# The hidden tiles of both FFNs start 128 bytes higher in SBUF

## The chip, the cores and the metric

The kernel runs on one core of one Trainium2 chip. The metric is the device time of one execution in microseconds (us); the number for the kernel before is the median of three runs. A profile of one execution gives the start and duration of every instruction on each engine: TensorE (PE for the matmuls, PEld for the weight loads), VectorE (DVE), ScalarE (ACT), GpSimd (POOL) and the queue that issues transfers (SP).

## What is computed

One layer of a hybrid streaming encoder on 512 tokens of width 1024, in float32. It is a macaron block: a half-weighted feed-forward network (FFN), a mixer with two kinds of attention heads, an output projection, a second half-weighted FFN, and a final norm.

```python
x = x + 0.5 * swiglu(rmsnorm(x, ffn1_norm), ffn1_w_gate, ffn1_w_up, ffn1_w_down)
proj = rmsnorm(x, mix_norm) @ w_in
...
x = x + concatenate([out_a, out_b]) @ w_out
x = x + 0.5 * swiglu(rmsnorm(x, ffn2_norm), ffn2_w_gate, ffn2_w_up, ffn2_w_down)
x = rmsnorm(x, final_norm)

def swiglu(h, w_gate, w_up, w_down):
    return (silu(h @ w_gate) * (h @ w_up)) @ w_down
```

The hidden width of an FFN is 2816, so it has 22 tiles of 128; the model width has 8 tiles of 128.

## The kernel before

Everything is held with features on the 128 partitions and the 512 tokens along the row, so that a tile of activations is 128 x 512 float32 values, 2,048 bytes in each partition. To keep float32 accuracy, each operand is split into a high and a low part (`xh`/`xl`, `x2h`/`x2l`, `h1h`/`h1l`, `h2h`/`h2l` for activations, `whi`/`wlo` for weights), and each product of 128 x 128 weights with 128 x 512 activations is three matmuls, issued by the helper `mm3` at lines 151 to 153: high x high, high x low and low x high (stationary x moving). The weights are the stationary operand, the activations the moving one (they stream through the array). In the projections `pj` (line 314), `uq` and `ukv` of the mixer it is the other way round: a 128-column piece of activations or latents stands still, and the weights move.

Weights arrive by transfer into `raw`, a block of up to 1,024 columns at a time; ScalarE makes `whi` (line 146), and GpSimd, or VectorE in a few places, makes `wlo` (line 147). Four buffers of each rotate.

The stages around the change, in the order of the program:

- FFN 1, gate and up (`gu`): for each of the 22 hidden tiles, 2 x 8 products on `xh`/`xl`, that is 1,056 matmuls. `gate` (lines 162 to 168) turns them into `h1h[f]`, `h1l[f]`.
- FFN 1, down (`dn`): for each of 8 output tiles, 22 products on `h1h`/`h1l`, 528 matmuls.
- The mixer: input projections `pj`, query and key/value projections `uq` and `ukv` from the latents `latT`, scores `s`, transposes `t` and `tr`, weighted values `pv`.
- The output projection (`wo`): 8 x 8 products on `xh`/`xl`, 192 matmuls.
- FFN 2, gate and up: 1,056 matmuls on `x2h`/`x2l`.
- FFN 2, down: as in FFN 1, but of its 22 hidden tiles only the first 14 are `h2h`/`h2l`; the last 8 are put into `xh`/`xl`, which are free by then. So one output tile is 42 matmuls on `h2` tiles, then 24 on `xh`/`xl`. The last output tile is done in two halves of 256 columns, which lets the final norm start early.

**Where the tiles lie.** Pools of SBUF are stacked in the order in which they are opened: `const`, `wpool`, `work`, `small`, and then, one after another at the same base, the pool of FFN 1 (`h1`), of the mixer (`mix`) and of the output projection with FFN 2 (`h2`). A tile takes its row in bytes, rounded up to 32. The tiles of `const` start at byte 16,512 of a partition. From there the sizes give, for the kernel before:

| tiles | first byte | remainder of 256 | remainder of 512 |
|---|---|---|---|
| `xh0` to `xl7` (16 tiles of 2,048) | 32,896 | 128 | 128 |
| `raw`, `whi`, `wlo` (4 buffers of 4,096 each) | 71,040, 87,424, 103,808 | 128 | 384 |
| `wa`, `wb`, `wc` of `work` (2,048 each) | 120,192 | 128 | 384 |
| first tile of `h1`, `mix` and `h2` | 132,864 | 0 | 256 |
| `h1h0`, `h1l0`, `h1h1`, ... and `x2h0`, ..., `x2l7`, `h2h0`, `h2l0`, ... (2,048 each) | from 132,864 | 0 | 256 |
| `latT` in `mix` (6 rows of 2,048) | 161,536 | 0 | 256 |

Within a weight tile, a block of 128 columns begins every 512 bytes. In the first projection of the mixer (416 columns) the second block of a weight tile begins 1,664 bytes on, which is 128 past a multiple of 256.

The order of instructions on each engine is set by a scheduler when the program is built.

Of the kernel before, what the change touches and what calls it, by code (L numbers as in the profile page):

```python
# [10 lines left out]
F32 = mybir.dt.float32  # L11
# [6 lines left out]
P = 128  # L18
# [5 lines left out]
NT = S // P  # L24
# [7 lines left out]

# columns of the packed parameter array
C_FFN1, C_MIX, C_FFN2, C_FINAL = 0, 8, 16, 24
# [5 lines left out]
def tile_macaron_block(  # L40
# [24 lines left out]

# [1 line left out]
    x = [const.tile([P, S], F32, name=f"x{k}") for k in range(KD)]  # L67
# [29 lines left out]

# [1 line left out]
    def split_x(k, c):  # L99
# [13 lines left out]
    def rsqrt(out, v, y, y2):  # L113
        """out = v^-1/2: by logarithm and exponential, then one Newton step."""
        act.activation(y, v, AF.Ln)
        act.activation(y, y, AF.Exp, scale=-0.5)
        dve.tensor_tensor(out=y2, in0=y, in1=y, op=ALU.mult)
        dve.tensor_tensor(out=y2, in0=y2, in1=v, op=ALU.mult)
        dve.tensor_scalar(out=y2, in0=y2, scalar1=-0.5, scalar2=1.5, op0=ALU.mult, op1=ALU.add)
        dve.tensor_tensor(out=out, in0=y, in1=y2, op=ALU.mult)  # L120

    def rstd_rows(ps):
        """rs[:, n] = (mean_d x[d, n]^2 + eps)^-1/2 on every partition."""
        sh = work.tile([P, S], F32R, tag="wa", name="sh")
        sl = work.tile([P, S], F32R, tag="wa", name="sl")
        act.copy(sh, ssum)
        dve.tensor_tensor(out=sl, in0=ssum, in1=sh.bitcast(F32), op=ALU.subtract)
        m = ps.tile([P, S], F32, tag="mm", name="ms")
        pe.matmul(m, lhsT=ones, rhs=sh, start=True, stop=False)
        pe.matmul(m, lhsT=ones, rhs=sl, start=False, stop=True)  # L130
        v = work.tile([P, S], F32, tag="wb", name="v")
        y = work.tile([P, S], F32, tag="wa", name="y")
        y2 = work.tile([P, S], F32, tag="wc", name="y2")
        dve.tensor_scalar(out=v, in0=m, scalar1=EPS, scalar2=None, op0=ALU.add)
        rsqrt(rs, v, y, y2)

    def wunit(src, n, lo_on=None, raw=None, step=1024):
        """A block of weights, split: hi + lo, both exact in 12 bits."""
        if raw is None:
            raw = wpool.tile([P, 1024], F32, tag="raw", name="raw")  # L140
            nc.sync.dma_start(out=raw[:, :n], in_=src)
        hi = wpool.tile([P, 1024], F32R, tag="whi", name="whi")
        lo = wpool.tile([P, 1024], F32R, tag="wlo", name="wlo")
        for c in range(0, n, step):
            cc = slice(c, min(n, c + step))
            act.copy(hi[:, cc], raw[:, cc])  # L146
            (lo_on or pool).tensor_tensor(out=lo[:, cc], in0=raw[:, cc], in1=hi[:, cc].bitcast(F32), op=ALU.subtract)  # L147
        return hi, lo
# [6 lines left out]
    def ffn(ps, gu, dn, H, XH, XL, after, raw0=None, squares=None, last=None):  # L155
        def gate(f, gup):
            """h = silu(g) u = (g / 2) (tanh(g / 2) + 1) u, split."""
            gs = work.tile([P, S], F32, tag="wa", name="gs")
# [54 lines left out]

    # =====================================================  FFN 1
    with tc.tile_pool(name="h1", bufs=1, reuse_waits="tile") as hp, \
            tc.tile_pool(name="ps1", bufs=8, space=PSUM, reuse_waits="tile") as ps:
        H = [(hp.tile([P, S], F32R, name=f"h1h{f}"), hp.tile([P, S], F32R, name=f"h1l{f}")) for f in range(NF)]
        # the tensor engine's clock rises while the first loads are under way
        warm = ps.tile([P, S], F32, tag="mm", name="warm")
# [16 lines left out]

    # =====================================================  mixer
    AH, AL = XH, XL
    with tc.tile_pool(name="mix", bufs=1, reuse_waits="tile") as mp:
# [14 lines left out]
        nc.sync.dma_start(out=rgain, in_=rope_gain)  # L254
        # rtab[:, q/k, t, :]: cos*g1, sin*g2, sin*g1, cos*g2
        rtmp = mp.tile([P, 2560], F32, tag="vAl", name="rtmp")
# [10 lines left out]
        def factors(ss, n, width, scaled, name):  # L267
            """ss [P, NT, n] sums of squares -> factors of the RMS norm, rtok folded in where scaled."""
            f = mp.tile([P, NT, n], F32, tag="f_" + name, name="f_" + name)
# [12 lines left out]
        def rope(dst, src, fac, i, n, tmp):  # L282
            """src [P, NT, n, 32] * fac -> normalised, rotated, into dst (gains in rtab)."""
            xn, a, b = tmp[:, :, :, 0:32], tmp[:, :, :, 32:48], tmp[:, :, :, 48:64]
# [12 lines left out]
        with tc.tile_pool(name="ps2", bufs=1, space=PSUM, reuse_waits="tile") as ps:  # L297
            NB = {"s": 2, "tr": 2, "t": 3, "pv": 1}

            def bank(group, i, name):  # L300
                """Bank i of one of the two groups of four."""
                tag = (("s",) * NB["s"] + ("tr",) * NB["tr"], ("t",) * NB["t"] + ("pv",) * NB["pv"])[group][i]
                return ps.tile([P, 512], F32, tag=tag, name=name, bufs=NB[tag])

            def in_proj(off, n, group):
                """The columns off.. of W_in for all tokens: four banks, one per token tile."""
                pts = [bank(group, t, "pj") for t in range(NT)]
# [9 lines left out]
            def sumsq(src, ss, nh, width):  # L317
                """ss[.., h] = sum of squares over each group of width columns of src."""
                sq = work.tile([P, 512], F32, tag="wb", name="sqp")
                sv = sq[:, :nh * width].rearrange("p (h w) -> p h w", w=width)  # L320
                act.activation(sv, src, AF.Square)
                dve.tensor_reduce(out=ss, in_=sv, op=ALU.add, axis=AX.X)

            # latents, with the token statistics
            pts = in_proj(0, LAT, 1)
# [44 lines left out]

            # B: queries from their latents
            qB = mp.tile([P, NT, NH, QK], F32, tag="qB", name="qB")
# [23 lines left out]

            # B: keys and values from their latents
            ssk = mp.tile([P, NT, NH], F32, tag="ssk", name="ssk")
# [26 lines left out]

# [1 line left out]
            def values_proj():  # L427
                """A: values."""
                VAh = mp.tile([P, NT, 4, 192], F32R, tag="vAh", name="VAh")
# [14 lines left out]
            def transposes(src):  # L444
                """The four token tiles of src(t) [128, n], transposed into one bank [n, 512]."""
                pt = ps.tile([P, 512], F32, tag="tr", name="tr", bufs=NB["tr"])
# [12 lines left out]
            def front(h):  # L459
                """Transposed, scaled and split queries and keys of a head (A: of its pair)."""  # L460
                if h < NH:
# [36 lines left out]
            def softmax(qh, ql, kh, kl, bias):  # L498
                """Probabilities of the query tiles 3..0, on 128 (i + 1) keys each."""
                pa = wpool.tile([P, 1024], F32, tag="raw", name="pa")  # L500
# [7 lines left out]
                for i, so in ((3, s3), (2, s2), (1, s01[:, 256:512]), (0, s01[:, 0:256])):  # L508
                    n = (i + 1) * P
# [10 lines left out]
            def flip(pi):  # L520
                """Probabilities with the keys on the partitions, split: keys 0 | keys 1 and keys 2 | keys 3."""
                t0 = ps.tile([P, 512], F32, tag="t", name="t0", bufs=NB["t"])
# [32 lines left out]

            # the stages of four neighbouring heads overlap
            shared["V"] = values_proj()
# [12 lines left out]

    # =====================================================  output projection, FFN 2, final norm
    with tc.tile_pool(name="h2", bufs=1, reuse_waits="tile") as hp, \
            tc.tile_pool(name="ps4", bufs=7, space=PSUM, reuse_waits="tile") as ps:
        X2H = [hp.tile([P, S], F32R, name=f"x2h{k}") for k in range(KD)]
        X2L = [hp.tile([P, S], F32R, name=f"x2l{k}") for k in range(KD)]
# [18 lines left out]

        # final norm: per half of the tokens, rstd as columns, spread over the partitions by the tensor engine
        mt = ps.tile([P, 512], F32, tag="mt", name="mt", bufs=1)
# [10 lines left out]
        def means(h):  # L607
            """The mean squares of these tokens in columns, with the last tile's part."""
            act.activation(sq[:, h], x[k7][:, h], AF.Square)
# [45 lines left out]
def _kxm(w, kt, m):  # L655
    """[kt*128, m] -> [128, kt, m]: the rows of each k tile on the partitions."""
    return w.reshape(kt, P, m).transpose(1, 0, 2)
# [10 lines left out]
def _layout(i):  # L668
# [16 lines left out]
    out["rope_tab"] = _rope_table()  # L685
    # the bias of query p and key column c of a tile whose last 128 columns are the query's own block
    rel = np.clip(np.arange(P)[:, None] + (S - P) - np.arange(S)[None, :], -128, 128) + 128
# [33 lines left out]
```

## Time and profile before

| what | value |
|---|---|
| median of three runs | 1017.27 us (1016.59 to 1018.25) |
| the profiled execution, first to last instruction (its own time; the page gives no other) | 1016.7 us |
| TensorE, matmuls | 993.1 us busy, 4579 instructions |
| TensorE, weight loads | 813.7 us |
| GpSimd | 591.5 us |
| VectorE | 397.3 us |
| ScalarE | 387.6 us |

A matmul's duration in the profile runs from its start to a modelled end behind the next one's start, so the durations of matmuls in a row overlap. How fast they follow one another is read from their starts, or from how many start in a stretch of known length. A window's count takes in an instruction that had begun before its edge.

### The profile page before, as it was taken

Reading aid. Unit: us, or ns where it says so; the run is one execution under the profiler, and the core shown is the slowest. Engines: PE = TensorE matmul, PEld = TensorE weight load, DVE = VectorE, ACT = ScalarE, POOL = GpSimd, SP = SyncE. Lnnn points to the kernel's source line nnn. Section 1 sums busy time; section 2 is a strip of 40 time slices with the busy share of each in tenths; the row PEclk is TensorE's granted clock in tenths of the full one; section 3 lists DMA queues with packets and bytes.
Section 4 is the critical chain, followed back from the end, with each engine's and each line's share of the span. In section 5 each row is a group of like instructions: output and inputs, shape, how many; then the busy total and the mean of one; then the engine's idle time right before and its main releaser. Section 6 shows DMA issues by size and latency. Waiting matters only on the chain.

```text
span 1016.7 us, 12060 instructions
## 1 busy us (share of the span) xinstructions
PE 993.1 (98%) x4579; PEld 813.7 (80%) x4579; DVE 397.3 (39%) x687; ACT 387.6 (38%) x648; POOL 591.5 (58%) x429
## 2 busy tenths in 40 slices
PE   7999999999999999898999999999999999999996
PEld 4888888888888889786778978888888888888886
DVE  7534324323121224776788845143333332200002
ACT  4433323323222225663678853343232332222220
POOL 7586676676555521285355567586666656645540
PEclk7999999999999999998999999999999999999999
DMA  5423323323333333220010062323322332333302
GB/s 201 151 83 105 104 83 104 104 83 94 97 94 93 91 110 104 83 62 1 21 43 2 1 208 86 101 84 103 95 92 86 101 102 80 90 103 94 99 16 83
DMA packets 28714, 89.90 MB, mean 88 GB/s; under 512 B 3440, under 2 KB 5616, under 8 KB 28656
## 3 DMA queue, kind: packets, MB, share of 16 engines
q1 hardware_dynamic: 27504, 88.08, 27.8%
q10 hardware_dynamic: 1152, 1.05, 0.3%
q8 instruction: 36, 0.59, 0.2%
q14 instruction: 22, 0.18, 0.1%
HBM read 87.02 MB, written 2.10 MB: 88 GB/s over the span
## 4 chain that ended last, share of the span: by engine, by line
PE 88%; DVE 4%; POOL 2%; issue 2%; ACT 1%; DMA 1%; POOLq 0%; DVEq 0%; ACTq 0%; SPq 0%
PE gu L153 16%; PE gu L152 16%; PE gu L151 16%; PE dn L151 8%; PE dn L152 8%; PE dn L153 8%; PE pj L153 2%; PE pj L151 2%; PE pj L152 2%; PE wo L153 1%; PE wo L152 1%; PE wo L151 1%; PE t L533 1%; PE s L151 1%; PE tr L448 1%
## 5 line engine op out<-in xcount | busy, mean ns | idle before, releaser
L147 POOL TENSOR_TENSOR wlo<-raw,whi 128x1024 fp32r<-128x1024 f32 x138 | 323.3, 2344 | 159.3 <-ACT whi L146 159.3
L146 ACT CAST whi<-raw 128x1024 fp32r<-128x1024 f32 (+3 forms) x165 | 167.3, 1014 | 468.1 <-PE gu L152 263.6
L152 PE MATMUL gu<-xl,whi 128*128 128x512 f32 x352 | 139.2, 396 | 3.0 <-DVE xl L101 2.9
L151 PE MATMUL gu<-xh,whi 128*128 128x512 f32 x352 | 138.3, 393 | 1.5 <-ACT whi L146 1.5
L151 PE MATMUL gu<-x2h,whi 128*128 128x512 f32 x352 | 139.0, 395 | 0.0
L153 PE MATMUL gu<-x2h,wlo 128*128 128x512 f32 x352 | 138.9, 395 | 0.0
L152 PE MATMUL gu<-x2l,whi 128*128 128x512 f32 x352 | 138.9, 395 | 0.0
L153 PE MATMUL gu<-xh,wlo 128*128 128x512 f32 x352 | 138.4, 393 | 0.2 <-DVE wlo L147 0.2
L166 POOL TENSOR_TENSOR us<-us,gs 128x512 f32<-128x512 f32 x44 | 58.4, 1329 | 111.8 <-DVE us L164 110.0
L165 DVE SCALAR_TENSOR_TENSOR gs<-th,gs 128x512 f32<-128x512 f32 x44 | 90.1, 2052 | 31.7 <-ACT th L163 31.7
L162 DVE TENSOR_TENSOR gs<-gu,rs 128x512 f32<-128x512 f32 x44 | 30.4, 691 | 178.5 <-PE gu L153 171.3
L199 DVE SCALAR_TENSOR_TENSOR x<-dn,x 128x512 f32<-128x512 f32 (+1 forms) x17 | 11.2, 661 | 198.9 <-PE dn L153 198.9
L152 PEld LDWEIGHTS gu<-xl,whi 128*128 128x128 f32 x352 | 66.6, 189 | 20.3 <-DVE xl L101 7.0
L151 PEld LDWEIGHTS gu<-xh,whi 128*128 128x128 f32 x352 | 66.8, 190 | 15.9 <-ACT whi L146 1.9
L151 PEld LDWEIGHTS gu<-x2h,whi 128*128 128x128 f32 x352 | 66.1, 188 | 16.1
L152 PEld LDWEIGHTS gu<-x2l,whi 128*128 128x128 f32 x352 | 66.1, 188 | 16.1
L153 PEld LDWEIGHTS gu<-x2h,wlo 128*128 128x128 f32 x352 | 66.1, 188 | 16.0
L153 PEld LDWEIGHTS gu<-xh,wlo 128*128 128x128 f32 x352 | 66.8, 190 | 14.5 <-DVE wlo L147 1.1
L153 PE MATMUL dn<-h1h,wlo 128*128 128x512 f32 x176 | 69.5, 395 | 0.0
L151 PE MATMUL dn<-h1h,whi 128*128 128x512 f32 x176 | 69.5, 395 | 0.0
L152 PE MATMUL dn<-h1l,whi 128*128 128x512 f32 x176 | 69.5, 395 | 0.0
L164 DVE SCALAR_TENSOR_TENSOR us<-gu,rs 128x512 f32<-128x512 f32 x44 | 30.4, 690 | 69.0 <-PE gu L153 65.5
(318 smaller groups left out, 1830.4 us busy)
## 6 DMA issues: line engine op xcount, KB each, us to landing
raw<-in_gu SPq DMA_DIRECT2D x87, 512.0 KB, 3.6
raw<-in_dn SPq DMA_DIRECT2D x32, 512.0 KB, 3.5
raw<-in_dn SPq DMA_DIRECT2D x16, 384.0 KB, 3.1
raw<-in_w_in SPq DMA_DIRECT2D x12, 512.0 KB, 3.5
raw<-in_w_out SPq DMA_DIRECT2D x8, 512.0 KB, 4.2
x<-in_xT SPq DMA_DIRECT2D x8, 256.0 KB, 5.2
bias<-in_bias_tab SPq DMA_DIRECT2D x8, 256.0 KB, 2.7
raw<-in_w_in SPq DMA_DIRECT2D x4, 416.0 KB, 3.4
```

Source lines behind the costliest of these rows:

```text
L146: act.copy(hi[:, cc], raw[:, cc])
L147: (lo_on or pool).tensor_tensor(out=lo[:, cc], in0=raw[:, cc], in1=hi[:, cc].bitcast(F32), op=ALU.subtract)
L151: pe.matmul(out, lhsT=ah, rhs=bh, start=start, stop=False)
L152: pe.matmul(out, lhsT=ah, rhs=bl, start=False, stop=False)
L153: pe.matmul(out, lhsT=al, rhs=bh, start=False, stop=stop)
L162: dve.tensor_tensor(out=gs, in0=gup[0], in1=rs, op=ALU.mult)
L164: dve.scalar_tensor_tensor(out=us, in0=gup[1], scalar=0.5, in1=rs, op0=ALU.mult, op1=ALU.mult)
L165: dve.scalar_tensor_tensor(out=gs, in0=th, scalar=1.0, in1=gs, op0=ALU.add, op1=ALU.mult)
L166: pool.tensor_tensor(out=us, in0=us, in1=gs, op=ALU.mult)
L199: dve.scalar_tensor_tensor(out=x[dt][:, h], in0=pt[:, h], scalar=0.5, in1=x[dt][:, h], op0=ALU.mult, op1=ALU.add)
L448: pe.transpose(pt[0:src(t).shape[1], t * P:(t + 1) * P], src(t), ident)
L533: pe.transpose(tt[:, o + i * P:o + (i + 1) * P], pi[i][:, j * P:(j + 1) * P], ident)
```

## The change

Each of the two pools gets a tile of 128 x 32 float32 values, 128 bytes in each partition, ahead of all its other tiles. Nothing reads or writes it. All other tiles of `h1` and `h2` thereby start 128 bytes higher, at remainder 128 of 256 and 384 of 512; `const`, `wpool`, `work`, `small` and `mix` stay where they are.

```diff
     with tc.tile_pool(name="h1", bufs=1, reuse_waits="tile") as hp, \
             tc.tile_pool(name="ps1", bufs=8, space=PSUM, reuse_waits="tile") as ps:
+        hp.tile([P, 32], F32, name="pad1")
         H = [(hp.tile([P, S], F32R, name=f"h1h{f}"), hp.tile([P, S], F32R, name=f"h1l{f}")) for f in range(NF)]
...
     with tc.tile_pool(name="h2", bufs=1, reuse_waits="tile") as hp, \
             tc.tile_pool(name="ps4", bufs=7, space=PSUM, reuse_waits="tile") as ps:
+        hp.tile([P, 32], F32, name="pad2")
         X2H = [hp.tile([P, S], F32R, name=f"x2h{k}") for k in range(KD)]
```

The diff removes comments too, which builds nothing. The lists of instructions of the two programs are the same on every engine, in the same order and with the same waits; only the addresses of the moved tiles differ.

## Rows read from the trace of the kernel before

**Rows 1.** The page: span, busy time of each engine.
```profile
span 1016.7 us, 12060 instructions
...
PE 993.1 (98%) x4579; PEld 813.7 (80%) x4579; DVE 397.3 (39%) x687; ACT 387.6 (38%) x648; POOL 591.5 (58%) x429
```

**Rows 2.** The page: the chain that ended last, by engine and by line.
```profile
PE 88%; DVE 4%; POOL 2%; issue 2%; ACT 1%; DMA 1%; POOLq 0%; DVEq 0%; ACTq 0%; SPq 0%
PE gu L153 16%; PE gu L152 16%; PE gu L151 16%; PE dn L151 8%; PE dn L152 8%; PE dn L153 8%; PE pj L153 2%; PE pj L151 2%; PE pj L152 2%; PE wo L153 1%; PE wo L152 1%; PE wo L151 1%; PE t L533 1%; PE s L151 1%; PE tr L448 1%
```

**Rows 3.** Timeline of TensorE, first matmuls of stages: start us, duration us.
```profile
255.71 0.40 PE L151 MATMUL dn<-h1h,whi 128*128 128x512 f32 x1
...
378.90 0.35 PE L151 MATMUL pj<-whi,xh 128*128 128x416 f32 x1
...
592.22 0.39 PE L151 MATMUL wo<-xh,whi 128*128 128x512 f32 x1
...
635.76 0.40 PE L151 MATMUL gu<-x2h,whi 128*128 128x512 f32 x1
...
882.62 0.40 PE L151 MATMUL dn<-h2h,whi 128*128 128x512 f32 x1
...
892.42 0.39 PE L151 MATMUL dn<-xh,whi 128*128 128x512 f32 x1
...
897.88 0.40 PE L151 MATMUL dn<-h2h,whi 128*128 128x512 f32 x1
...
989.36 0.28 PE L151 MATMUL dn<-h2h,whi 128*128 128x256 f32 x1
```

**Rows 4.** Windows in FFN 1 and FFN 2 gate/up: engines' busy us (instructions).
```profile
core 0: us, PE busy (x) PEld busy (x) DVE busy (x) ACT busy (x) POOL busy (x), PEclk, DMA share, GB/s
100.00:200.00 100.00, 100.00 (x443) 82.84 (x442) 35.81 (x28) 30.13 (x36) 67.01 (x37) 1.00 0.29 95
680.00:780.00 100.00, 100.00 (x431) 80.44 (x430) 33.39 (x27) 30.15 (x36) 68.25 (x38) 1.00 0.31 95
```

**Rows 5.** Groups by form, whole span: busy us, mean ns of one | idle before.
```profile
L151 PE MATMUL gu<-x2h,whi 128*128 128x512 f32 x352 | 139.0, 395 | 0.0
...
L151 PE MATMUL dn<-h1h,whi 128*128 128x512 f32 x176 | 69.5, 395 | 0.0
...
L151 PE MATMUL dn<-h2h,whi 128*128 128x512 f32 x98 | 38.7, 395 | 0.0
...
L151 PE MATMUL dn<-xh,whi 128*128 128x512 f32 x56 | 21.8, 389 | 0.0
```

**Rows 6.** Groups by form from 435 to 441.8 us, then from 403 to 419 us.
```profile
L151 PE MATMUL ukv<-whi,latT 128*128 128x512 f32 x4 | 1.6, 400 | 0.0
L153 PE MATMUL ukv<-whi,latT 128*128 128x512 f32 x4 | 1.6, 397 | 0.0
L152 PE MATMUL ukv<-wlo,latT 128*128 128x512 f32 x4 | 1.6, 394 | 0.0
...
L153 PE MATMUL pj<-whi,xl 128*128 128x512 f32 x25 | 9.6, 389 | 0.0
```

**Rows 7.** Timeline of the 416-column projection: starts of its second and third block.
```profile
381.14 0.36 PE L151 MATMUL pj<-whi,xh 128*128 128x416 f32 x1
...
383.42 0.35 PE L151 MATMUL pj<-whi,xh 128*128 128x416 f32 x1
```

**Rows 8.** Timeline of the output projection: its seventh matmul.
```profile
593.61 0.39 PE L151 MATMUL wo<-xh,whi 128*128 128x512 f32 x1
```

**Rows 9.** Timeline of the last output tile's first half: its change of tiles, and its end.
```profile
994.39 0.28 PE L151 MATMUL dn<-xh,whi 128*128 128x256 f32 x1
...
997.27 0.28 PE L151 MATMUL dn<-h2h,whi 128*128 128x256 f32 x1
```

**Rows 10.** Groups by form of GpSimd: the low parts of hidden tiles.
```profile
L168 POOL TENSOR_TENSOR h1l<-us,h1h 128x512 fp32r<-128x512 f32 x22 | 28.6, 1298 | 0.0
...
L168 POOL TENSOR_TENSOR xl<-us,xh 128x512 fp32r<-128x512 f32 x8 | 10.4, 1297 | 0.0
```

**Rows 11.** Timeline of one head's scores: two of its three matmuls of 512 columns.
```profile
499.25 0.39 PE L152 MATMUL s<-xl,xh 64*128 64x512 f32 x1
499.48 0.39 PE L153 MATMUL s<-xh,xl 64*128 64x512 f32 x1
```

## The prediction

> **What bounds the kernel now.** I read the page's first parts, then the chain that ended last, then TensorE's start times stage by stage. TensorE is busy for 993.1 of 1016.7 us [rows 1], and the chain runs on it for 88% of the span, with gate/up at 16% for each of its three lines and down at 8% for each [rows 2]. Its idle time before these matmuls is 0.0. So an FFN stage lasts as long as its number of matmuls times the distance from one start to the next ("spacing" below). Durations overlap, since one matmul's modelled end lies after the next start, so I work from starts and counts.
>
> Most of these stages run the same instruction: 128x512 moving columns against a 128x128 block of split weights, at full clock, nothing waiting. Yet the spacing has two values. FFN 1 down starts at 255.71 and the next stage at 378.90; 8 x 22 x 3 = 528 matmuls in 123.19 us are 233.3 ns each. The output projection takes 43.54 us for its 192: 226.8 ns. FFN 2 gate/up takes 246.86 us for 1058 (1056 and two of the mean): 233.3 ns [rows 3]. FFN 1 gate/up starts 443 in a stretch of 100 us, so (100 + 0.39) / 443 = 226.6 ns; FFN 2 gate/up starts 431, so 232.9 ns [rows 4]. (Each count takes in one matmul of 0.39 us that had begun before the edge.)
>
> The clearest place is FFN 2 down. One output tile is one accumulation, with one kind of weight tile and one PSUM bank. Its first 42 matmuls read `h2` tiles and its last 24 read `xh`/`xl` in their role as the last eight hidden tiles. The first 42 take 892.42 - 882.62 = 9.80 us, 233.3 ns each; the 24 take 5.46 us, 227.5 ns; then the next tile begins with the long spacing again [rows 3]. The durations say the same: 395 ns for `x2h`, `h1h`, `h2h`, 389 ns for `xh` [rows 5]. Engines, clock and weights do not differ there; what differs is which tile streams through.
>
> **What the change does.** It adds one tile of 128 bytes ahead of each pool of hidden tiles. No instruction is added and none changes place or wait on any engine, so every term is a price of an address. From the layout table: weights and `xh`/`xl` start 128 bytes past a multiple of 256; `h1`, `x2`, `h2` start on a multiple; after the change all of them start 128 past one. All inner offsets of the FFN operands (512 bytes for a weight block, 2,048 for a tile) keep this. The pairs with the short spacing thus agree modulo 256, those with the long spacing are 128 apart, and the change makes all agree.
>
> A second kind of pair that is 128 apart is the key/value projection: weights stream from `whi`/`wlo`, and `latT`, which starts on a multiple of 256, stands still. Its durations are 400, 394 and 397 ns, where the neighbouring projection, with `xh` standing still, has 389 when left alone [rows 6]. So it is not the streamed tile's address alone; the pair counts. A third kind is the 416-column projection, where every second block of moving weights begins 1,664 bytes on, which shifts the pair by 128 modulo 256: the first block's 12 matmuls take 381.14 - 378.90 = 2.24 us (187 ns), the second's 383.42 - 381.14 = 2.28 us (190 ns) [rows 3, 7]. That is the right sign, but later blocks differ by less and one not at all.
>
> **The sum.** For the short spacing I take the 226.8 ns of the output projection, which has its settling in: its first six matmuls take 593.61 - 592.22 = 1.39 us, 231.7 ns each, before the short spacing holds [rows 3, 8].
> FFN 1 down: 528 x (233.3 - 226.8) ns = 3.4 us.
> FFN 2 gate/up: 1056 x 6.5 ns = 6.9 us.
> FFN 2 down, the seven output tiles that run whole: 7 x 42 = 294, x 6.5 ns = 1.9 us.
> FFN 2 down, last tile in halves of 256 columns: no gain. 42 on `h2` take 994.39 - 989.36 = 5.03 us (119.8 ns), 24 on `xh` 997.27 - 994.39 = 2.88 us (120.0 ns) [rows 3, 9].
> The 168 full-width down matmuls on `xh` may come from 227.5 to 226.8 ns, 0.1 us; left out.
> Everything else reads tiles that stay. The engines that write the moved tiles show no price of place: GpSimd's subtraction into `h1l` takes 1298 ns and into `xl`, on the other side of the 128 bytes, 1297 ns [rows 10].
> Total 12.2 us.
>
> What could take the gain's place? GpSimd makes the low half of the weights; it is busy for 67.01 of 100 us while FFN 1 gate/up already runs at 226.6 ns with TensorE never idle, and for 68.25 in FFN 2 gate/up [rows 4]. At the faster pace that becomes about 70. DMA, at a share of 0.31, has more room. So no other engine becomes the bound, and the 12.2 us should reach the end. The profile's own time is 1016.7 us, 0.6 under the median of 1017.27. From 1016.7 - 12.2 = 1004.5, the median after should be about 1005.0.
>
> [...] The rows show 233.3 and 226.8 ns for one form, with the place as the difference [rows 3]. [...]
>
> **The rivals.**
> *It is the region, not the 128 bytes: no change, 1017.3 us.* All pairs with the long spacing have one operand in the upper part of the partition (from byte 132,864: `h1`, `x2`, `h2`, `latT`), and all with the short spacing have both below it. Then a shift of 128 bytes moves nothing across the line. For it: rows 3 and 6 fit as well as they fit mine. Against it: in rows 7 both operands are low, and still 190 stands beside 187; that is little.
> *The pair now meets too exactly: slower, about 1026.7 us.* Modulo 512 the pairs with the short spacing lie 256 apart, the others 128 or 384, and after the change the moved tiles lie exactly on the weights' remainder (384 and 384), which no long run of the trace has. If places repeat every 512 bytes, this could be the worst position, not the best. The nearest rows for a bad position are the key/value projection's longest: 400 ns against 395, so 5 ns more than now, x 1878 matmuls = 9.4 us, 1017.3 + 9.4 = 1026.7. It decides once the spacing rises over 234.4 ns (0.2% is 2.0 us, / 1878 = 1.1 ns). The only rows with equal remainders at this width are the score matmuls of the first heads, three in a row: 499.48 - 499.25 = 0.23 us [rows 11]. That is neither the short spacing nor worse than now, and three are too few, since the output projection needs six to settle.
> *A tile's place costs nothing, and the spacing has another cause: no change, 1017.3 us.* The cause would have to follow the stage or the engines beside it. Against it: the spacing steps within one accumulation, where only the streamed tile changes [rows 3]. [...]
> *A part only.* The moved tiles may settle at a spacing between the two; half of the gain would give 1011.
>
> **How the numbers follow.** My forecast gets 0.65: agreement modulo 256 is the plainest rule that sorts all rows. A part of the gain over 0.2% gets 0.05, the region 0.15, a place that costs nothing 0.04, slower 0.11. So faster 0.70, same 0.19, slower 0.11; 0.2%, 2.0 us, is about what the measurement can tell, for the three runs before span 1.66 us. The forecast's own range is 1003.2 to 1007: the low end takes 226.6 ns and a run 1 us under the median, the high end 1 ns less gain on each of 1878 matmuls. It holds too little alone, so the range reaches through the partial gain and the unchanged time, 1003.2 to 1017.9, and leaves out the slower case and the unchanged time's upper edge.
>
> **What would show it.** Right: `gu<-x2h` and `dn<-h1h`, `dn<-h2h` at 389 ns instead of 395; 441 or more starts per 100 us in FFN 2 gate/up and FFN 1 down; within one FFN 2 output tile no step between the hidden tiles of the two kinds; GpSimd busy at about 70% in FFN 2 gate/up; FFN 1 gate/up and the output projection unchanged. The gain stands at FFN 1 down's end as 3.4 us and at FFN 2 down's start as 10.3 us. Wrong: the moved tiles still at 395 (region), or over it (the 512-byte rival), or the spacing falls and TensorE then idles on `whi` or `wlo`.

## The result and the profile after

The kernel after takes 1004.86 us (median of four runs, 1004.16 to 1005.59), the kernel before 1017.38 (1016.59 to 1018.25): a ratio of 0.9879 [0.9865, 0.9893], 12.5 us less. The forecast was 1005.0.

The page of the kernel after, as in [rows 1, 2]: span, busy time of each engine, and the chain that ended last, by engine.
```profile
span 1003.2 us, 12060 instructions
...
PE 979.7 (98%) x4579; PEld 813.2 (81%) x4579; DVE 395.9 (39%) x687; ACT 387.5 (39%) x648; POOL 590.5 (59%) x429
...
PE 89%; DVE 4%; issue 2%; POOL 2%; ACT 1%; DMA 1%; SPq 0%; POOLq 0%; DVEq 0%; ACTq 0%
```
As many instructions as before, TensorE still busy for 98% of the span, and 13.4 us less on TensorE alone; the other engines' busy times hardly move.

The timeline of the kernel after has the starts of the stages, as [rows 3] has them for before (columns: start us, duration us, engine, line, operation).
```profile
255.99 0.39 PE L151 MATMUL dn<-h1h,whi 128*128 128x512 f32 x1
...
375.67 0.35 PE L151 MATMUL pj<-whi,xh 128*128 128x416 f32 x1
...
587.48 0.40 PE L151 MATMUL wo<-xh,whi 128*128 128x512 f32 x1
...
631.01 0.39 PE L151 MATMUL gu<-x2h,whi 128*128 128x512 f32 x1
...
870.85 0.39 PE L151 MATMUL dn<-h2h,whi 128*128 128x512 f32 x1
...
880.37 0.39 PE L151 MATMUL dn<-xh,whi 128*128 128x512 f32 x1
...
885.81 0.39 PE L151 MATMUL dn<-h2h,whi 128*128 128x512 f32 x1
...
975.57 0.28 PE L151 MATMUL dn<-h2h,whi 128*128 128x256 f32 x1
```
FFN 1 down takes 375.67 - 255.99 = 119.68 us for its 528 matmuls, 226.7 ns each. FFN 2 gate/up takes 239.84 us for 1058, again 226.7 ns. In the first output tile of FFN 2 down, the 42 matmuls on `h2` take 9.52 us and the 24 on `xh`/`xl` 5.44 us: 226.7 ns for both, and the step inside the tile is gone.

Windows of the kernel after: us, then busy time and count of each engine, granted TensorE clock, DMA share, GB/s. The first and third stretch answer to [rows 4]; the second lies in FFN 1 down.
```profile
100.00:200.00 100.00, 100.00 (x442) 82.78 (x442) 35.84 (x28) 30.13 (x36) 67.20 (x37) 1.00 0.28 96
270.00:370.00 100.00, 100.00 (x442) 82.78 (x442) 21.72 (x16) 27.55 (x34) 49.64 (x24) 1.00 0.33 97
680.00:780.00 100.00, 100.00 (x443) 82.84 (x442) 34.79 (x28) 31.77 (x38) 67.85 (x39) 1.00 0.30 99
```
Three stages with 442 or 443 starts per 100 us, where FFN 2 gate/up had 431, and TensorE is busy for all 100 us, so no other engine has become the bound.

The groups by form of the kernel after, as [rows 5]: busy us, mean ns of one, idle before.
```profile
L151 PE MATMUL gu<-x2h,whi 128*128 128x512 f32 x352 | 136.9, 389 | 0.0
...
L151 PE MATMUL dn<-h1h,whi 128*128 128x512 f32 x176 | 68.5, 389 | 0.0
...
L151 PE MATMUL dn<-h2h,whi 128*128 128x512 f32 x98 | 38.1, 389 | 0.0
```
The three groups on hidden tiles now read 389 ns, as `dn<-xh` did all along [rows 5].

**Where the time went, stage by stage**, from the starts here and in [rows 3]:

| stage | before, us | after, us | difference |
|---|---|---|---|
| up to FFN 1 down | 255.71 | 255.99 | +0.28 |
| FFN 1 down | 123.19 | 119.68 | -3.51 |
| mixer | 213.32 | 211.81 | -1.51 |
| output projection | 43.54 | 43.53 | -0.01 |
| FFN 2 gate/up | 246.86 | 239.84 | -7.02 |
| FFN 2 down, seven whole tiles | 106.74 | 104.72 | -2.02 |
| the rest | 27.34 | 27.63 | +0.29 |

The three stages of the change give 12.55 us. The profiled spans differ by 13.5, because the mixer, in which no tile has moved, is 1.5 us shorter in this execution. Up to the first transposes `tr` the two mixers are alike: 97.91 us before (the transposes begin at 476.81) and 97.88 after (at 473.55). The rest takes 115.41 and 113.93 us, and there the clock differs. In both kernels TensorE stands idle for 4.0 us ahead of these transposes, and towards the end of that the granted clock falls from 1.00 to 0.50. It stays there for about 6.8 us in this execution of the kernel before and for about 3.4 us in that of the kernel after. At 0.50 the 512-column matmuls of `pj` start every 0.43 us, at 1.00 every 0.23. Windows within the low stretch, first before, then after:
```profile
476.10:482.70 6.60, 5.89 (x18) 5.06 (x19) 2.66 (x4) 1.37 (x2) 0.00 (x0) 0.50 0.00 0
...
473.70:476.80 3.10, 3.10 (x12) 2.81 (x13) 1.60 (x3) 1.37 (x2) 0.00 (x0) 0.50 0.00 0
```
The 3.5 us by which these two windows differ can cost up to 1.75 us at half the clock (an estimate from these rows), which is enough for the difference. It does not go with the moved tiles: the kernels of experiments 1, 5 to 7 and 9 leave the mixer's tiles in place too, and their mixers take 209.99 to 213.10 us. The medians, 12.5 us apart, agree with the three stages.

### The profile page after: what moved, and what is told of

Same layout as the page of the kernel before. It is cut to its first block, busy times and chain, and to the rows that moved or that the text cites. A ratio compares the mean times of both kernels' runs of the same rounds, so it can differ in the third digit from the quotient of the medians.

```text
span 1003.2 us, 12060 instructions
## 1 busy us (share of the span) xinstructions
PE 979.7 (98%) x4579; PEld 813.2 (81%) x4579; DVE 395.9 (39%) x687; ACT 387.5 (39%) x648; POOL 590.5 (59%) x429
## 4 chain that ended last, share of the span: by engine, by line
PE 89%; DVE 4%; issue 2%; POOL 2%; ACT 1%; DMA 1%; SPq 0%; POOLq 0%; DVEq 0%; ACTq 0%
PE gu L152 16%; PE gu L153 16%; PE gu L151 16%; PE dn L151 8%; PE dn L152 8%; PE dn L153 8%; PE pj L153 2%; PE pj L151 2%; PE pj L152 2%; PE t L534 2%; PE wo L152 1%; PE wo L153 1%; PE wo L151 1%; PE s L151 1%; PE tr L449 1%
## 5 line engine op out<-in xcount | busy, mean ns | idle before, releaser
L151 PE MATMUL gu<-x2h,whi 128*128 128x512 f32 x352 | 136.9, 389 | 0.0
L153 PE MATMUL gu<-x2h,wlo 128*128 128x512 f32 x352 | 136.8, 389 | 0.0
L152 PE MATMUL gu<-x2l,whi 128*128 128x512 f32 x352 | 136.8, 389 | 0.0
L151 PEld LDWEIGHTS gu<-xh,whi 128*128 128x128 f32 x352 | 66.8, 190 | 15.5 <-ACT whi L146 1.1
L164 DVE SCALAR_TENSOR_TENSOR us<-gu,rs 128x512 f32<-128x512 f32 x44 | 30.3, 690 | 65.2 <-PE gu L153 65.2
```

The lines of the kernel that those rows point to most:

```text
L151: pe.matmul(out, lhsT=ah, rhs=bh, start=start, stop=False)
L152: pe.matmul(out, lhsT=ah, rhs=bl, start=False, stop=False)
L153: pe.matmul(out, lhsT=al, rhs=bh, start=False, stop=stop)
L164: dve.scalar_tensor_tensor(out=us, in0=gup[1], scalar=0.5, in1=rs, op0=ALU.mult, op1=ALU.mult)
```

## The experiments

The theory (call it the pair): what counts is that the streamed tile and the stationary weights agree in their first byte modulo 256. Its rivals: the streamed tile's own remainder counts; an empty tile ahead of a pool is enough; the part of SBUF counts; the period is 512 bytes; any nearer place helps. The region is out by the result alone: the moved tiles still lie above byte 132,864 and have the short spacing, 226.7 ns. In the same way the 512-byte form of the slower rival is out: moved tiles and weights now agree modulo 512 too, and that is the short spacing. Each diff below is against the kernel after.

**1. FFN 2 moved by 256 bytes in place of 128.** FFN 1 keeps its 128.
```diff
-        hp.tile([P, 32], F32, name="pad2")
+        hp.tile([P, 64], F32, name="pad2")
```


> FFN 1's pad stays at 128 bytes, FFN 2's becomes 256. If the spacing goes by whether the streamed and the standing tile start at the same remainder of 256: FFN 1 down takes 119.7 us (226.7 ns a matmul), FFN 2 gate/up 246.9 us (233.3 ns) as in the kernel before, and the time is 1017.4 - 3.5 = 1013.9 us. If any pad ahead of the pool would do, or the distance from the pool's base: both FFNs at 226.7 ns and 1004.9 us.

Measured: 1014.44 us (1013.02 to 1015.04), ratio 0.9964 [0.9951, 0.9977]. Timeline of this kernel: the starts of four stages.
```profile
255.12 0.39 PE L151 MATMUL dn<-h1h,whi 128*128 128x512 f32 x1
...
374.80 0.35 PE L151 MATMUL pj<-whi,xh 128*128 128x416 f32 x1
...
631.43 0.40 PE L151 MATMUL gu<-x2h,whi 128*128 128x512 f32 x1
...
878.29 0.40 PE L151 MATMUL dn<-h2h,whi 128*128 128x512 f32 x1
```
FFN 2 gate/up is back at 246.86 us, to the hundredth what it was before, although the pool has an empty tile ahead of it, and a larger one. FFN 1 down stays at 119.68 us: one half of the change alone, worth 3.7 us in the ratio against the term of 3.4. A shift by a whole 256 bytes leaves this stage at 233.3 ns, so here the place repeats every 256 bytes; 128 is not a period, since 128 bytes more than in the kernel before gave 226.7 ns.

**2. Everything moved to remainder 0.** On top of the change, 128 bytes ahead of all tiles of `const`: `xh`/`xl`, the weights and the hidden tiles all start on a multiple of 256. (To make room in the mixer's pool, two small tiles of sums share one buffer, here and in experiments 3, 4 and 8.)
```diff
+    const.tile([P, 32], F32, name="pad0")
     x = [const.tile([P, S], F32, name=f"x{k}") for k in range(KD)]
```


> Every tile of the kernel after moves up by 128 bytes more, so that weights, xh/xl and hidden tiles all start at remainder 0 of 256, where only the hidden tiles stood before. If the pair's agreement counts: every FFN stage at 226.7 ns and 1004.9 us, as after. If the streamed tile's own remainder (128 good, 0 bad) counts: FFN 1 gate/up (1056), FFN 1 down (528), the output projection (192), FFN 2 gate/up (1056), FFN 2 down (462) and the projections of 512 columns (288) all at 233.3 ns, 3582 x 6.6 ns = 23.6 us more than after, 1028.5 us.

Measured: 1004.48 us (1003.87 to 1005.62), ratio 0.9871 [0.9856, 0.9885]. The same three windows of this kernel:
```profile
100.00:200.00 100.00, 100.00 (x443) 82.86 (x442) 35.08 (x28) 30.86 (x38) 67.33 (x37) 1.00 0.29 99
270.00:370.00 100.00, 100.00 (x443) 82.87 (x442) 21.74 (x16) 27.56 (x34) 50.09 (x25) 1.00 0.33 95
680.00:780.00 100.00, 100.00 (x443) 82.84 (x442) 34.56 (x28) 30.87 (x37) 68.28 (x38) 1.00 0.30 96
```
The hidden tiles start where they cost 233.3 ns in the kernel before, as far as remainders go, and cost 226.7 now. So it is not their own remainder alone that counts, but its agreement with the weights'.

**3. Only the weights moved.** No empty tile in the FFN pools, one at the end of `const`: the weights go to remainder 0, `xh`/`xl` stay at 128, and the pools above the weights go to 128 with the shift. So every FFN pair is 128 apart, those of FFN 1 gate/up and the output projection for the first time.
```diff
+    const.tile([P, 32], F32, name="padw")
...
-        hp.tile([P, 32], F32, name="pad1")
...
-        hp.tile([P, 32], F32, name="pad2")
```


> No pads in the FFN pools; 128 bytes ahead of the weight buffers, which moves everything above them too: weights at remainder 0, xh/xl and hidden tiles at 128. If the pair counts: every 512-column matmul of the FFNs, the output projection and the projections on xh/xl is 128 bytes off and takes 233.3 ns; beside the kernel before, FFN 1 gate/up loses 1056 x 6.6 = 7.0 us, the output projection 1.3, FFN 2 down's part on xh/xl 1.1, the projections 288 x 6.6 = 1.9: 1017.4 + 11.3 = 1028.7 us. If the streamed tile's own remainder counts: all at 226.7 ns, 1004.9 us.

Measured: 1023.83 us (1021.72 to 1024.46), ratio 1.0056 [1.0041, 1.0071]. The windows of this kernel, and below them two of its groups by form.
```profile
100.00:200.00 100.00, 100.00 (x432) 81.16 (x431) 33.79 (x27) 30.14 (x36) 65.36 (x36) 1.00 0.28 95
270.00:370.00 100.00, 100.00 (x432) 81.14 (x431) 18.51 (x13) 25.61 (x32) 51.66 (x25) 1.00 0.32 90
680.00:780.00 100.00, 100.00 (x432) 81.09 (x432) 32.69 (x28) 30.75 (x37) 69.71 (x39) 1.00 0.30 95
```
```profile
L152 PE MATMUL gu<-x2h,whi 128*128 128x512 f32 x352 | 138.9, 395 | 0.0
...
L152 PE MATMUL wo<-xh,whi 128*128 128x512 f32 x64 | 25.3, 395 | 0.0
```
FFN 1 gate/up falls from 443 starts to 432, and the output projection's groups from 389 to 395 ns, with tiles that have not moved. That settles the pair against the tile. The size came out smaller than expected: the spacing is 232.4 ns in all these stages, 5.7 above the short one and not 6.6, and the hidden stages, still 128 apart, went from 233.3 to 232.4. So from before, FFN 1 gate/up gives +6.6 us, the output projection +1.1, FFN 1 down and FFN 2 gate/up -0.5 and -1.0, the mixer -0.8, the rest +0.6: 6.0 in the profiled span, 6.2 in the medians (the kernel before had 1017.62 beside this run). The 1028.7 us expected were 4.9 too many, since the price came out smaller and the projections' 1.9 us do not show in the mixer's total.

**4. The mixer's pool moved too.**
```diff
+        mp.tile([P, 32], F32, tag="pad3", name="pad3")
         qA = mp.tile([P, NT, 512], F32, tag="qA", name="qA")
```


> The kernel after with 128 bytes ahead of the mixer's pool too, so that latents, keys and values also agree with the weights and queries. If the pair counts also where a tile stands still: the key/value projection's 24 matmuls come from some 234 to some 230 ns or less where they run in a row, the 72 of 512 columns in scores and weighted values a little too; 0.2 to 0.8 us in all, 1004.1 to 1004.7 us, hardly to be told from after. If these stages end on other waits: 1004.9 us.

Measured: 1004.38 us (1003.49 to 1005.09), ratio 0.9866 [0.9849, 0.9882], not to be told from the kernel after. But the groups by form of the key/value projection show it. First the kernel after (from 430 to 440 us), where `latT` and the weights are 128 apart as in [rows 6], then this one (from 435 to 442 us), where they agree.
```profile
L151 PE MATMUL ukv<-whi,latT 128*128 128x512 f32 x4 | 1.6, 400 | 0.0
L153 PE MATMUL ukv<-whi,latT 128*128 128x512 f32 x4 | 1.6, 397 | 0.0
L152 PE MATMUL ukv<-wlo,latT 128*128 128x512 f32 x4 | 1.6, 394 | 0.0
```
```profile
L152 PE MATMUL ukv<-wlo,latT 128*128 128x512 f32 x5 | 1.9, 389 | 0.0
L153 PE MATMUL ukv<-whi,latT 128*128 128x512 f32 x4 | 1.6, 389 | 0.0
L151 PE MATMUL ukv<-whi,latT 128*128 128x512 f32 x4 | 1.6, 389 | 0.0
```
Over the whole span the eight matmuls of each line have means of 393 to 399 ns in the kernel after; here the 13 in the window have 389 in all three lines. So the rule holds in these rows with weights streaming and latents standing still; there are only too few such matmuls for the total.

**5 to 7. Other distances.** Each kernel moves the two pools by other amounts: 32 and 64 bytes, 96 and 160, 192 and 224. The first as a diff; the others differ in the two sizes.
```diff
-        hp.tile([P, 32], F32, name="pad1")
+        hp.tile([P, 8], F32, name="pad1")
...
-        hp.tile([P, 32], F32, name="pad2")
+        hp.tile([P, 16], F32, name="pad2")
```
32 and 64 bytes:

> Pads of 32 bytes in FFN 1 and 64 in FFN 2: the hidden tiles start 96 and 64 bytes below the weights' remainder of 256. If only exact agreement gives the short spacing: 233.3 ns in FFN 1 down and FFN 2 gate/up, 1017.4 us. If the price falls with the distance: FFN 1 down near 231.6 ns, FFN 2 near 230 ns, about 1012 us. [...]

96 and 160 bytes:

> Pads of 96 bytes in FFN 1 and 160 in FFN 2: 32 below and 32 above agreement. If only exact agreement gives the short spacing: 233.3 ns in both, 1017.4 us. If the price falls with the distance: near 228.3 ns in both, about 1008 us. If agreement within some distance is enough: 226.7 ns in both, 1004.9 us. If the sign counts, the two FFNs differ.

192 and 224 bytes:

> Pads of 192 bytes in FFN 1 and 224 in FFN 2: 64 and 96 above agreement. If only exact agreement gives the short spacing: 233.3 ns in both, 1017.4 us. If the price grows with the distance on both sides: near 230 ns in FFN 1 down, 231.6 ns in FFN 2, about 1013 us.

Measured: 1016.76 us, ratio 0.999 [0.9977, 1.0003]; 1017.96, 0.9998 [0.9987, 1.0009]; 1015.48, 0.9982 [0.9971, 0.9993]. Timeline of the second: FFN 1 down with 96 bytes, 32 short of agreement, and FFN 2 gate/up with 160, 32 past it.
```profile
255.64 0.40 PE L151 MATMUL dn<-h1h,whi 128*128 128x512 f32 x1
...
378.85 0.35 PE L151 MATMUL pj<-whi,xh 128*128 128x416 f32 x1
...
634.94 0.40 PE L151 MATMUL gu<-x2h,whi 128*128 128x512 f32 x1
...
881.79 0.39 PE L151 MATMUL dn<-h2h,whi 128*128 128x512 f32 x1
```
123.21 and 246.85 us: the full price, 32 bytes from agreement on either side. Groups by form of the third kernel, whose 192 bytes put FFN 1's hidden tiles 64 past agreement:
```profile
L151 PE MATMUL dn<-h1h,whi 128*128 128x512 f32 x176 | 69.3, 394 | 0.0
L153 PE MATMUL dn<-h1h,wlo 128*128 128x512 f32 x176 | 69.0, 392 | 0.0
L152 PE MATMUL dn<-h1l,whi 128*128 128x512 f32 x176 | 68.3, 388 | 0.0
```
One of the three kinds reads as in agreement, and the spacing is 228.9 ns (120.87 us for the stage), the lowest without agreement at 512 columns in all runs. FFN 2 gate/up has 233.3 ns, the full price. So neither expectation holds for both stages: FFN 1 down is nearer the price that grows with the distance (230 ns), FFN 2 gate/up is at that of exact agreement.

**8. Only `wlo` moved.** The two weight tiles now disagree with each other: `wlo` at remainder 0; `whi`, `xh`/`xl` and, by the shift, the hidden tiles at 128.
```diff
+    gap = []
...
+        if not gap:
+            gap.append(wpool.tile([P, 32], F32, tag="gap", name="gap", bufs=1))
         lo = wpool.tile([P, 1024], F32R, tag="wlo", name="wlo")
...
-        hp.tile([P, 32], F32, name="pad1")
...
-        hp.tile([P, 32], F32, name="pad2")
```


> The hidden tiles agree with whi and xh/xl as after, but the low weights wlo start 128 bytes off all of them, in every FFN stage and the output projection. A weight tile is loaded while the matmul before it streams. If the price is paid by the matmul that streams while a weight tile 128 bytes off is loaded, only the second of each three (xl or low part streaming, wlo loading) pays, and the mean spacing is 226.7 + 6.6/3 = 228.9 ns; if it is paid by the matmul that uses the weights that are off, the third pays, with the same mean. 3294 matmuls x 2.2 ns = 7.3 us over after: 1012.2 us. If one pair that is off breaks the short spacing for all three: 233.3 ns, 3294 x 6.6 = 21.8 us, 1026.7 us.

Measured: 1020.30 us (1017.94 to 1021.01), ratio 1.0028 [1.0015, 1.0042]. Groups by form in FFN 2 gate/up of this kernel; the three lines of `mm3` are 155 to 157 here, issued in this order.
```profile
L157 PE MATMUL gu<-x2h,wlo 128*128 128x512 f32 x352 | 139.6, 397 | 0.0
...
L156 PE MATMUL gu<-x2l,whi 128*128 128x512 f32 x352 | 139.2, 396 | 0.0
L155 PE MATMUL gu<-x2h,whi 128*128 128x512 f32 x352 | 136.9, 389 | 0.0
```
The second of three pays although it multiplies by `whi`, with which it agrees: while it streams, the next weights, `wlo`, are loaded. The timeline of this kernel shows both start together (PEld is the weight load):
```profile
700.28 0.40 PE L156 MATMUL gu<-x2l,whi 128*128 128x512 f32 x1
700.28 0.19 PEld L157 LDWEIGHTS gu<-x2h,wlo 128*128 128x128 f32 x1
```
The third pays too: it multiplies by `wlo`, and the next load, of `whi`, agrees with it. So neither the load under way nor a matmul's own weights explain it alone; two of three pay, 231.1 ns in the mean. That is 4.4 ns over the short spacing, and 3294 times that on top of the kernel after would be 1019.4 us; neither expected figure, 1012.2 or 1026.7, came. Either both count, or a disturbed matmul also delays the one behind it; this run cannot tell these apart.

**9. Eight and sixteen bytes.** FFN 1's hidden tiles are cut from one large tile, 16 bytes past agreement; `x2` in the same way, 8 bytes past it; `h2` stays in agreement.
```diff
-        H = [(hp.tile([P, S], F32R, name=f"h1h{f}"), hp.tile([P, S], F32R, name=f"h1l{f}")) for f in range(NF)]
+        hall = hp.tile([P, 2 * NF * S + 8], F32R, name="h1all")
+        H = [(hall[:, 4 + 2 * f * S:4 + (2 * f + 1) * S], hall[:, 4 + (2 * f + 1) * S:4 + (2 * f + 2) * S]) for f in range(NF)]
...
-        X2H = [hp.tile([P, S], F32R, name=f"x2h{k}") for k in range(KD)]
+        xall = hp.tile([P, 2 * KD * S + 64], F32R, name="x2all")
+        X2H = [xall[:, 2 + k * S:2 + (k + 1) * S] for k in range(KD)]
...
```


> The kernel after, with the hidden tiles of FFN 1 cut from one big tile 16 bytes past agreement, and x2 of FFN 2 8 bytes past it; h2 stays in agreement. If agreement must be exact: 233.3 ns in FFN 1 down and FFN 2 gate/up, 1004.9 + 3.5 + 7.0 = 1015.4 us. If some bytes are allowed: 226.7 ns in one or both, 1004.9 us with both. FFN 2 down stays at 226.7 ns either way.

Measured: 1014.19 us (1013.85 to 1015.39), ratio 0.9972 [0.996, 0.9984]. Timeline of this kernel:
```profile
255.58 0.39 PE L151 MATMUL dn<-h1all,whi 128*128 128x512 f32 x1
...
377.90 0.35 PE L151 MATMUL pj<-whi,xh 128*128 128x416 f32 x1
...
633.42 0.40 PE L151 MATMUL gu<-x2all,whi 128*128 128x512 f32 x1
...
880.25 0.40 PE L151 MATMUL dn<-h2h,whi 128*128 128x512 f32 x1
```
Eight bytes cost the whole price in FFN 2 gate/up (246.83 us, 233.3 ns), sixteen most of it in FFN 1 down (231.7 ns). So agreement has no free zone of 8 bytes on the upper side; on the lower side the nearest distance tried is 32. The tiles moved here are also the only FFN tiles in all runs that do not start on a multiple of 32 bytes. A price of such a start by itself would look the same, and no run tells the two apart.

All distances together (hidden tile's first byte less the weights', modulo 256):

| distance | FFN 1 down, ns | FFN 2 gate/up, ns |
|---|---|---|
| -128 (before) | 233.3 | 233.3 |
| -96 | 234.3 | |
| -64 | | 233.3 |
| -32 | 233.3 | |
| 0 (after) | 226.7 | 226.7 |
| +8 | | 233.3 |
| +16 | 231.7 | |
| +32 | | 233.3 |
| +64 | 228.9 | |
| +96 | | 233.3 |
| +128 (256 bytes) | | 233.3 |

Only -128 and 0 were tried in both stages, so a difference between the columns can come from the distance or from the stage.

## Why the prediction was right

**The bound and the rule.** That an FFN stage is its count of matmuls times their spacing, and that the spacing hangs on the pair's agreement modulo 256, held for matmuls of 512 columns in the result and in experiments 1, 2, 3 and 4, each of which could have broken it. The "region" and the "meets too exactly" rivals fell with the result itself. That a place costs nothing fell too: programs alike in order and waits differ by 12.5 us, and the same `xh` tiles go from 389 to 395 ns when the weights move and they do not (experiment 3).

**The terms.** 3.4, 6.9 and 1.9 us were forecast, 3.51, 7.02 and 2.02 measured. The first two are about 0.1 us low, because the 226.8 ns of the output projection include its first six longer matmuls [rows 8]; 226.7 ns would have given 3.5 and 7.0, and still 1.9 for the third. What the third lacks is the 0.1 us that the sum left out, for the down matmuls on `xh` behind the `h2` ones. The halves of 256 columns gained nothing, as forecast: the first 42 on `h2` take 5.03 us as before (975.57 to 980.60). At FFN 1 down's end the profiles are 378.90 - 375.67 = 3.23 us apart, for 3.4 forecast, because the stage itself began 0.28 us later; at FFN 2 down's start the profiles are 882.62 - 870.85 = 11.77 us apart, not 10.3, and the mixer's 1.5 is the difference. Two slips of the working cost nothing. The sum sets the profile's span beside the median as if they were one kind of time; the execution profiled after has a span of 1003.2 us and a time of 1004.98, so the span is 1.8 us short of the time, but the offset drops out of the difference. And the low end of the range, written as 1003.2 us, comes to 1017.27 - 12.6 - 1 = 1003.7 from the median and its own terms.

**What was weak.** The 416-column projection was read as a sign for the rule [rows 7]: 187 ns in its first block, 190 in its second. In the kernel after, where none of its tiles has moved, the timeline has the second to fifth block begin here:
```profile
377.91 0.34 PE L151 MATMUL pj<-whi,xh 128*128 128x416 f32 x1
...
380.15 0.35 PE L151 MATMUL pj<-whi,xh 128*128 128x416 f32 x1
...
382.42 0.35 PE L151 MATMUL pj<-whi,xh 128*128 128x416 f32 x1
...
384.69 0.35 PE L151 MATMUL pj<-whi,xh 128*128 128x416 f32 x1
```
The second block, 128 apart, now takes 2.24 us like the first, and the third, which agrees, takes 2.27 like the fourth, which does not. So at 416 columns agreement does not sort the blocks, and the only evidence offered against the region rival was none; the forecast was righter than its argument there. Nor is it scatter: in the four kernels whose FFN 1 down has the short spacing (after, experiments 1, 2 and 4) each block whose starts were read repeats to 0.01 us, the second at 2.23 to 2.24, and in the kernel before the second takes 2.28 us with the same tiles. What differs there is the stage just ahead, FFN 1 down; no run tests how that carries over.

The row on equal remainders [rows 11] was weak as well: 0.23 us, from times rounded to 0.01, cannot tell 226.7 from 233.3 ns. GpSimd was forecast at about 70% in FFN 2 gate/up and is at 67.85 in the window. Over the whole stage it is busy for 160.86 of 246.86 us before and 160.28 of 239.84 after, 65.2% and 66.8%: the same work in less time, as argued, from a window that lay above the stage's mean. And the price of disagreement, taken as one figure in the expectation of experiment 3, is not one.

**What stays open** is the mechanism behind the rule. The runs show that matmuls of 512 columns follow each other more slowly when weights and stream start at different remainders (228.9 to 234.3 ns against 226.7), and experiment 8 that the weights loaded next count too, or that a slowed matmul slows the one behind it (396 and 397 ns against 389). Why FFN 2 gate/up pays 6.6 ns at every distance tried, while FFN 1 down pays 2.2 to 7.6, and why moving the weights gives 5.7 for the same 128 bytes, no run explains. The price is no fixed addition to each matmul either. By the starts in the traces, to the nanosecond, FFN 1 down of the kernel before has spacings of about 238 and 229 ns in turn, and experiment 7's has 232, 226 and 229.

The rule is not shown for narrower matmuls. At 256 columns it even fails: with the kernel of 160 bytes (experiment 6), whose `h2` tiles lie 32 past agreement, the first half of the last output tile has its 42 matmuls on `h2` between these two starts:
```profile
988.67 0.28 PE L151 MATMUL dn<-h2h,whi 128*128 128x256 f32 x1
...
993.57 0.28 PE L151 MATMUL dn<-xh,whi 128*128 128x256 f32 x1
```
That is 4.90 us, 116.7 ns each, against 5.03 us, 119.8 ns, both in agreement and 128 apart.

## What to carry to other kernels

Where TensorE never idles and one form of matmul shows two spacings (here 226.7 and 233.3 ns), sort the groups by the addresses of both operands before looking for a wait: here the table of first bytes modulo 256 was enough. For matmuls of 512 columns, each with its own weight load, lay out pools so that streamed and stationary tiles start at the same remainder of 256; here one empty tile of 128 bytes ahead of each pool did it, worth 12.5 us, and a change of a size can undo it: with 256 bytes FFN 2 gate/up was back at 246.86 us (experiment 1). Take the price from the row that is longest undisturbed, and test a rule on every block of its kind, and on other widths, before two blocks of eight count as evidence.

## What the runs showed of the hardware

Agreement is worth 226.7 against 233.3 ns per matmul of 512 columns with its own weight load, at a granted clock of 1.00, in FFN 1 down and FFN 2 gate/up of the kernels after and before. In FFN 2 gate/up 8 bytes of distance cost the same 6.6 ns as 128 (experiment 9). The weight loads themselves do not grow in the records of these two kernels: 80.44 us for 430 of them, 187 ns each, in [rows 4], and 82.84 for 442, 187 ns, after. No placing tried brought a stage of 512 columns below 226.7 ns; at 256 columns the shortest of the spacings read, 116.7 ns, stands 32 bytes out of agreement (experiment 6).
